# The place of one power on GpSimd's queue in the opening of a decoder layer

## The chip, the cores and the metric

The kernel runs on one core of a Trainium2 chip. The metric is the device time of one execution in microseconds (us). A core has five engines that each work through a queue of their own in order: TensorE (PE; its weight loads are listed as PEld), VectorE (DVE), ScalarE (ACT), GpSimd (POOL) and SyncE (SP), which issues most of the DMA transfers. Engines wait for each other by semaphores.

## The reference

One layer of a hybrid decoder on 256 tokens of width 1024, all in float32: two token mixers side by side on a normalised input, a gated merge, cross attention to 256 memory tokens, a gated MLP, and a last norm.

```python
xn = rmsnorm(h, norm_mix_g[l])
q_a, k_a, v_a, q_b, f_b, i_b, og_b, g_a, g_b = split_cols(xn @ w_in[l])
y_a = moba_attention(q_a, k_a, v_a, positions) @ w_br_attn[l]
y_b = hgrn2(q_b, f_b, i_b, og_b, lb_all[l], hgrn_norm_g[l]) @ w_br_hgrn[l]
merged = jax.nn.sigmoid(g_a) * y_a + jax.nn.sigmoid(g_b) * y_b
h = h + merged @ w_out[l]
h = h + memory_cross_attention(rmsnorm(h, norm_x_g[l]), rmsnorm(mem, norm_mem_g[l]),
                               wq_x[l], wkv_x[l], wo_x[l])
hn = rmsnorm(h, norm_ffn_g[l])
gu = hn @ w_ffn_in[l]
h = h + (jax.nn.silu(gu[..., :FFN_HIDDEN]) * gu[..., FFN_HIDDEN:]) @ w_ffn_out[l]
```

Two pieces matter here. `rmsnorm` multiplies each token by the reciprocal root of its mean square (its rstd), `x * rsqrt(mean(x*x) + 1e-6)`. The attention rotates its queries and keys by `cos` and `sin` of `position * inv_freq` (the rotary tables). The recurrence (`hgrn2`) has a forget gate `lb + (1 - lb) * sigmoid(f_b)`.

## The kernel before, in words

**Weights.** All weights lie in device memory as 97 units of 128 x 2048 values (1 MB), in the order in which they are used. `prep` takes one unit: SyncE loads it into `raw` (two buffers), ScalarE rounds it to `hi` (L189, in two halves of 128 x 1024; three buffers), and `lo = raw - hi` is made at L193, by VectorE alone for units 0 to 8 and from unit 9 on by VectorE (576 of 1024 columns) and GpSimd (448). A product with a weight takes three matmuls: hi with the high part of the input, lo with the high part, and hi with the low part (L233 to L235). `nxt` returns the next unit and prepares two more ahead of it. A raw buffer is free once the unit's lo is done, a hi buffer once TensorE has used it.

**Order.** TensorE's order is the program's. GpSimd's is the program's too in the region from the rotary generator's start to the end of the q gate (`manual_schedule` of Pool); elsewhere a scheduler orders the queues when the program is built. Work that runs beside the products is written as generators: `start` puts one on a list, and `tick`, called after each unit of a product, runs each of them up to its next `yield`.

**The opening.** Units 0 to 3 make the forget gate f: four accumulators `psg` (two column halves by two token halves of 128). The input's gain is applied, but not its rstd, as that is a factor for each token: it is applied where a product is read. To get it, ScalarE squares the tokens (H, loaded by SyncE) with a sum into `ssqx` (L516), VectorE makes mean + eps (`v_`, L282), and GpSimd raises it to the power -0.5 (L284, result `r_x`). VectorE halves it (`r_half`, L521), and ScalarE's tanh (`fth`, L467, four of them, one for each accumulator) reads an accumulator with it. TensorE turns the tanhs into `fT` (transposes, L445), and goes on with unit 4, the first of the q gate (accumulators `pst`, units 4 to 7), whose four evictions are `qth`. Then come `Vb` and `va` (units 8 to 15), and the attention's q and k, whose evictions (L725) read the rotary tables Ct and St.

**The rotary generator** `rope_tables` runs on GpSimd in parts with a `yield` between: the angle and its first reduction by multiples of 2 pi; a second part of five multiply-adds (`acc`, each L368 and L369) and a rounding (`rnd`, L363 to L365); a third of seven multiply-adds and some comparisons; a fourth of five operations; then four bare yields, two sines on ScalarE (L398, L399) and eight products with `r_x` that fill Ct and St (L403 to L405). The program drives the generator by hand at first: two `next` before the products, two more right behind the power,

```python
r_x = rstd_of(ssqx, "x")
next(rt)
next(rt)
r_half = cp.tile([128, 2], F32, name="r_half")
```

and then by ticks of the q gate, four in all, until `drain(rt)` ahead of the attention's q. GpSimd's products of neighbouring decays (Tt, L572) come behind the rotary chain in its queue.

Of the kernel before, what the change touches and what calls it, by code (L numbers as in the profile page):

```python
# [115 lines left out]
def build(tc, A, out):  # L116
    nc = tc.nc
    V, SC, G, PE, SY = nc.vector, nc.scalar, nc.gpsimd, nc.tensor, nc.sync
    with ExitStack() as ctx:
# [20 lines left out]
        def small(name, shape):  # L140
            return sp.tile([128] + list(shape), F32, name=name)
# [212 lines left out]
        def rope_tables():  # L354
            posf = small("posf", [2])
            G.tensor_copy(posf, posi)
            q = cp.tile([128, 7, 2, 32], F32, name="rt")
            ang, m, mh, ml, r, t, u = (q[:, i] for i in range(7))
            for i in range(2):
                G.tensor_scalar(ang[:, i], ifq, posf[:, i:i + 1], None, op0=ALU.mult)  # L360

            def rnd(o, src, c):
                G.tensor_scalar(o, src, c, None, op0=ALU.mult)  # L363
                G.tensor_scalar(o, o, RND, None, op0=ALU.add)
                G.tensor_scalar(o, o, RND, None, op0=ALU.subtract)  # L365

            def acc(o, a, c, b):
                G.tensor_scalar(u, a, float(c), None, op0=ALU.mult)  # L368
                G.tensor_tensor(o, u, b, op=ALU.add)  # L369

            rnd(m, ang, 1.0 / (TWO_PI * 1024.0))
            rnd(mh, m, 1.0 / 1024.0)
            G.tensor_scalar(mh, mh, 1024.0, None, op0=ALU.mult)
            G.tensor_tensor(ml, m, mh, op=ALU.subtract)
            yield 1
            acc(r, mh, -D1, ang)
            acc(r, ml, -D1, r)
            acc(r, mh, -D2, r)
            acc(t, ml, -D2, r)
            acc(t, mh, -D3, t)  # L380
            rnd(t, t, 1.0 / TWO_PI)
            yield 1
            for a, c in ((t, C1), (ml, D2), (mh, D3), (t, C2), (ml, D3), (t, C3), (m, D4)):
                acc(r, a, -c, r)
            lim = 3.1415925
            G.tensor_scalar(t, r, lim, -TWO_PI, op0=ALU.is_gt, op1=ALU.mult)
            G.tensor_scalar(ml, r, -lim, TWO_PI, op0=ALU.is_lt, op1=ALU.mult)
            G.tensor_tensor(r, r, t, op=ALU.add)
            G.tensor_tensor(r, r, ml, op=ALU.add)
            yield 1  # L390
            G.tensor_scalar(r, r, lim, -lim, op0=ALU.min, op1=ALU.max)
            G.tensor_scalar(t, r, 0.0, -2.0, op0=ALU.is_gt, op1=ALU.mult)
            G.tensor_scalar(t, t, 1.0, None, op0=ALU.add)
            G.tensor_tensor(t, t, r, op=ALU.mult)
            G.tensor_scalar(t, t, TWO_PI / 4, None, op0=ALU.add)
            for _ in range(4):
                yield 1
            tc.keep_in_program_order(SC.activation(m, r, AF.Sin))  # L398
            tc.keep_in_program_order(SC.activation(mh, t, AF.Sin))  # L399
            for i in range(2):  # L400
                rs = r_x[:, i:i + 1]
                for c in range(2):
                    G.tensor_scalar(Ct[:, i, c * 32:(c + 1) * 32], mh[:, i], rs, None, op0=ALU.mult)  # L403
                G.tensor_scalar(St[:, i, 0:32], m[:, i], rs, -1.0, op0=ALU.mult, op1=ALU.mult)
                G.tensor_scalar(St[:, i, 32:64], m[:, i], rs, None, op0=ALU.mult)  # L405

        rt = rope_tables()
        region = tc.manual_schedule(engines={mybir.EngineType.Pool})
        region.__enter__()
# [778 lines left out]
```

## Time and profile before

| | us |
|---|---|
| median of three runs | 632.65 |
| lowest and highest run | 631.9 and 633.71 |
| the profiled execution | 634.07 |
| its span, first to last instruction | 632.3 |
| mean granted TensorE clock | 0.994 |

A line of a timeline gives start and length in us, the engine, the line of the kernel, the operation, out<-in with partitions x elements, and how many instructions are merged; in brackets stands how long the engine was idle before and what ended that. A line of the chain gives start, length and what ran. A line of waits gives who waited for whom, the total in us, how often, and the longest. A line of stretches gives the stretch, its length, busy time and instructions of each engine asked for (PE, PEld, DVE, ACT, POOL), the granted clock as a share of full speed, the DMA engines' busy share and GB/s. Times count from the start of the span.

### The profile page before, as it was taken

What the parts mean: (1) busy time and instruction counts of PE and PEld (TensorE: products, weight loads), DVE (VectorE), ACT (ScalarE), POOL (GpSimd) and SP (SyncE); (2) the same over time, 40 slices, a digit from 0 to 9 for tenths busy, and PEclk for the clock granted to TensorE, in tenths of its full rate; (3) what the DMA queues carried; (4) which work ended last, traced back from release to release, by engine and by line L of the source; (5) the groups of instructions that cost most, each with busy time, mean ns of one, the idle gap of its engine ahead of it and who ended that gap; (6) DMA issues with size and microseconds to landing.
All of it is one profiled execution on the core that took longest, in us unless ns stands there. A gap on an engine that the chain in (4) does not pass through costs nothing.

```text
span 632.3 us, 8666 instructions
## 1 busy us (share of the span) xinstructions
PE 620.0 (98%) x3262; PEld 521.5 (82%) x3262; DVE 384.8 (61%) x649; ACT 325.1 (51%) x513; POOL 366.7 (58%) x287
## 2 busy tenths in 40 slices
PE   8899999999999999999999999999999999999995
PEld 6778888888887887778889999888888888888884
DVE  6475778889856875784656456754444444444433
ACT  5585544433377666773355444644544444444433
POOL 1897553466534564356865866646556655566542
PEclk9989999999999999999999999999999999999998
DMA  8655354443334433535454554562354554455511
GB/s 292 274 201 200 134 168 165 168 165 134 134 135 152 158 98 130 209 136 209 175 199 145 189 200 140 210 217 101 123 181 194 199 194 171 179 191 199 201 66 66
DMA packets 17321, 107.52 MB, mean 170 GB/s; under 512 B 2304, under 2 KB 2688, under 8 KB 4864
## 3 DMA queue, kind: packets, MB, share of 16 engines
q1 hardware_dynamic: 16704, 106.42, 47.1%
q10 hardware_dynamic: 576, 0.55, 0.3%
q8 instruction: 25, 0.41, 0.3%
q14 instruction: 16, 0.13, 0.1%
HBM read 105.92 MB, written 1.05 MB: 169 GB/s over the span
## 4 chain that ended last, share of the span: by engine, by line
PE 94%; issue 3%; POOL 2%; ACT 1%; DVE 0%; POOLq 0%; ACTq 0%
PE pst L233 14%; PE pst L235 14%; PE pst L234 14%; PE psi L233 6%; PE psi L235 6%; PE psi L234 6%; PE acc L235 3%; PE acc L234 3%; PE acc L233 3%; PE psf L229 2%; PE psf L228 2%; PE psf L230 2%; PE lp L600 2%; PE pso L233 1%; PE pso L235 1%
## 5 line engine op out<-in xcount | busy, mean ns | idle before, releaser
L193 POOL TENSOR_TENSOR lo<-raw,hi 128x448 fp32r<-128x448 f32 x172 | 269.9, 1583 | 196.7 <-ACT hi L189 193.7
L189 ACT ACTIVATE hi<-raw 128x1024 fp32r<-128x1024 f32 (+1 forms) x194 | 195.8, 1036 | 184.8 <-PE pst L235 67.8
L193 DVE TENSOR_TENSOR lo<-raw,hi 128x576 fp32r<-128x576 f32 (+2 forms) x194 | 198.1, 1028 | 126.5 <-ACT hi L189 125.3
L233 PE MATMUL pst<-hi,Xh 128*128 128x512 f32 x256 | 103.8, 406 | 0.0
L234 PE MATMUL pst<-lo,Xh 128*128 128x512 f32 x256 | 100.4, 392 | 0.0
L235 PE MATMUL pst<-hi,Xl 128*128 128x512 f32 x256 | 100.4, 392 | 0.0
L233 PE MATMUL psi<-hi,h2h 128*128 128x512 f32 x176 | 69.6, 395 | 0.0
L235 PE MATMUL psi<-hi,h2l 128*128 128x512 f32 x176 | 68.6, 390 | 0.0
L234 PE MATMUL psi<-lo,h2h 128*128 128x512 f32 x176 | 68.6, 390 | 0.0
L235 PEld LDWEIGHTS pst<-hi,Xl 128*128 128x128 f32 x256 | 48.5, 189 | 10.4
L233 PEld LDWEIGHTS pst<-hi,Xh 128*128 128x128 f32 x256 | 48.4, 189 | 10.0 <-issue 0.7
L234 PEld LDWEIGHTS pst<-lo,Xh 128*128 128x128 f32 x256 | 48.6, 190 | 9.2
L235 PEld LDWEIGHTS psi<-hi,h2l 128*128 128x128 f32 x176 | 33.0, 188 | 7.0
L233 PEld LDWEIGHTS psi<-hi,h2h 128*128 128x128 f32 x176 | 33.1, 188 | 6.6
L234 PEld LDWEIGHTS psi<-lo,h2h 128*128 128x128 f32 x176 | 33.1, 188 | 6.5
L233 PE MATMUL acc<-hi,hid 128*128 128x512 f32 x88 | 34.3, 390 | 0.0
L234 PE MATMUL acc<-lo,hid 128*128 128x512 f32 x88 | 34.2, 389 | 0.0
L235 PE MATMUL acc<-hi,hid 128*128 128x512 f32 x88 | 34.2, 389 | 0.0
L1075 DVE SCALAR_TENSOR_TENSOR fu<-psi,r_h,fg 128x256 f32<-128x256 f32 x22 | 10.6, 483 | 26.0 <-ACT fg L1073 26.0
L1073 ACT ACTIVATE fg<-psi,r_h 128x256 f32<-128x256 f32 x22 | 10.4, 475 | 29.9 <-PE psi L235 29.9
L235 PEld LDWEIGHTS acc<-hi,hid 128*128 128x128 f32 x88 | 16.5, 188 | 3.4
L234 PEld LDWEIGHTS acc<-lo,hid 128*128 128x128 f32 x88 | 16.5, 188 | 3.4
(338 smaller groups left out, 1174.5 us busy)
## 6 DMA issues: line engine op xcount, KB each, us to landing
raw<-w SPq DMA_DIRECT2D x95, 1024.0 KB, 4.8
raw<-w SPq DMA_DIRECT2D x8, 256.0 KB, 5.1
H<-xtok SPq DMA_DIRECT2D x1, 1024.0 KB, 9.4
mraw<-mT SPq DMA_DIRECT2D x1, 1024.0 KB, 7.0
out<-H SPq DMA_DIRECT2D x4, 256.0 KB, 2.2
xraw<-xT SPq DMA_DIRECT2D x2, 256.0 KB, 4.3
gfin<-gfin SPq DMA_DIRECT2D x1, 512.0 KB, 5.0
xraw<-xT ACTq DMA_DIRECT2D x2, 128.0 KB, 4.9
```

The source lines that it names most:

```text
L189: SC.activation(hi[:, a], raw[:, a], AF.Copy)
L193: eng.tensor_tensor(lo[:, b], raw[:, b], hi[:, b].bitcast(F32), op=ALU.subtract)
L228: PE.matmul(ps, lh, rh, start=first, stop=False)
L229: PE.matmul(ps, lh, rl, start=False, stop=False)
L230: PE.matmul(ps, ll, rh, start=False, stop=last)
L233: PE.matmul(ps, xh, h, start=first, stop=False)
L234: PE.matmul(ps, xh, l, start=False, stop=False)
L235: PE.matmul(ps, xl, h, start=False, stop=last)
L600: PE.matmul(ps[:, j], KS[:, a0 + j], QQ[:, a0 + j], start=True, stop=True)
L1073: SC.activation(g, ps[:, 0:256], AF.Silu, scale=r)
L1075: V.scalar_tensor_tensor(u, ps[:, 256:512], r, g, op0=ALU.mult, op1=ALU.mult)
```

## The change

One `yield` is put into the rotary generator behind the second of the five multiply-adds of its second part. The generator so has one part more. The two `next` ahead of the products now end behind two multiply-adds; the power of the tokens' rstd follows in GpSimd's queue; and the two `next` behind it run the other three multiply-adds with the rounding, and the third part. The parts that the ticks run come one tick later each: the sines and the tables Ct and St come with the first tick of `Vb` instead of the last of the q gate. The numbers of lines behind the yield grow by one.

```diff
             yield 1
             acc(r, mh, -D1, ang)
             acc(r, ml, -D1, r)
+            yield 1
             acc(r, mh, -D2, r)
             acc(t, ml, -D2, r)
             acc(t, mh, -D3, t)
             rnd(t, t, 1.0 / TWO_PI)
             yield 1
```

## The prediction

> **What bounds the kernel now.** I read the busy time of each engine first, then what TensorE waited for over the whole span.
>
> ```profile
> PE 620.0 (98%) x3262; PEld 521.5 (82%) x3262; DVE 384.8 (61%) x649; ACT 325.1 (51%) x513; POOL 366.7 (58%) x287
> PE fT__408 L445 <- ACT fth L467: 2.3, 2, 2.1
> PE warm L321 <- DVE still L318: 1.6, 1, 1.6
> PE psg L504 <- ACT hi L189: 0.7, 1, 0.7
> PE psg L504 <- ACT Xh L326: 0.3, 1, 0.3
> ```
>
> TensorE is busy 98% of the span, and the list of its waits has four entries in all, each of them in the opening. The largest, 2.3 us, is the first transposes of the forget gate (tiles fT), which wait for ScalarE's tanh (fth). After it TensorE waits for nobody, so every microsecond taken out here should come out of the end. Next I read the chain of work that ended last around that wait, and the timeline of each engine on it.
>
> ```profile
> 27.66 0.37 POOL rt L365
> 28.03 0.70 POOL r_x L284
> ...
> 32.23 0.55 PE fT__408 L445 x3
> ```
>
> ```profile
> 23.76 0.32 POOL L369 TENSOR_TENSOR rt<-rt 128x64 f32<-128x64 f32 x1
> ...
> 27.99 0.73 POOL L284 TENSOR_TENSOR r_x<-v__339,nhalf 128x2 f32<-128x2 f32 x1
> ```
>
> ```profile
> 24.04 0.17 DVE L282 TENSOR_SCALAR v__339<-ssqx 128x2 f32<-128x2 f32 x1 [1.85 <-ACT junk L516]
> 28.75 0.17 DVE L521 TENSOR_SCALAR r_half<-r_x 128x2 f32<-128x2 f32 x1 [4.54 <-POOL r_x L284]
> ```
>
> ```profile
> 23.83 0.19 ACT L516 ACTIVATION_READ_ACCUMULATOR junk<-H 128x1 f32 x1
> 29.02 0.69 ACT L467 ACTIVATE fth<-psg,r_half 128x512 f32<-128x512 f32 x1 [5.01 <-DVE r_half L521]
> 29.60 1.99 ACT L189 ACTIVATE hi<-raw 128x1024 fp32r<-128x1024 f32 x2
> 31.50 1.83 ACT L467 ACTIVATE fth<-psg,r_half 128x512 f32<-128x512 f32 x3
> ```
>
> The chain runs through GpSimd's rotary line (rt), the power (r_x), VectorE's halving of it (r_half) and the tanh. The power's input v is there at 24.04 + 0.17 = 24.21, but the power starts at 27.99: it stands in GpSimd's queue behind the second part of the rotary chain, and ScalarE idles 5.01 us for it. So 3.78 us of the latency of r_x is queueing alone.
>
> **The change, part by part.** No instruction is added or removed. The second part of the chain has five multiply-add pairs (L368, L369) and one rounding (L363 to L365). The new yield stands after the first two pairs, the second of which ends at 23.76 + 0.32 = 24.08. The power now follows, and the other three pairs and the rounding come behind it.
>
> *The power.* GpSimd gets to it at 24.08 and waits for v until 24.21, so it idles some 0.15 us; behind it in that queue stand only the remaining rotary operations. With 0.04 us to pass on (23.83 + 0.19 to 24.04 shows 0.02), the power runs 24.25 to 24.98. The first tanh came 29.02 - 27.99 = 1.03 after the power's start, so it starts at 25.28, 3.74 us earlier.
>
> *ScalarE behind it.* Its order stays: a tanh, two roundings of weight unit 4 (hi), then the three other tanhs. The transposes need the first two tanhs. The roundings need unit 4's weights.
>
> ```profile
> 19.65 0.33 SPq L183 DMA_DIRECT2D raw<-w  x1
> raw<-w SPq DMA_DIRECT2D x1, 1024.0 KB, 6.1
> 29.19 0.39 PE L235 MATMUL psg<-hi,Xl 128*128 128x512 f32 x1
> 30.68 2.48 DVE L193 TENSOR_TENSOR lo<-raw,hi 128x1024 fp32r<-128x1024 f32 x2 [1.76 <-ACT hi L189]
> ```
>
> The weights land at 19.65 + 6.1 = 25.75, just ahead of the rounding at 25.28 + 0.58 = 25.86. The second tanh, 31.50 - 29.02 = 2.48 after the first, starts at 27.76 and ends near 28.45. TensorE's last matmul of the f gate starts at 29.19 whatever happens here, so its transposes could start at 29.42: a spare of about 1 us, and the wait goes whole. What is late next is the fourth tanh: it needs that same matmul, so ScalarE waits until about 29.6 with the eviction of fT and unit 5's rounding behind it. ScalarE ends the tanhs near 30.3 instead of 33.33, some 3.0 us earlier. VectorE's lo of unit 4 (30.68, 1.08 after its first rounding) starts at 26.94 and is done by 29.42, before TensorE's first use.
>
> *TensorE.* Here I count by stretches: the columns are length, busy (instructions), granted clock, and DMA; the last row is one microsecond of the second stretch with all five engines, where the clock stands behind them.
>
> ```profile
> 29.42:32.96 3.54, 1.22 (x9) 1.00 0.00 0
> 32.96:40.15 7.19, 7.19 (x28) 0.76 0.60 218
> 40.15:40.94 0.79, 0.79 (x10) 1.00 1.10 467
> 40.94:51.92 10.98, 10.98 (x51) 1.00 0.59 210
> ```
>
> ```profile
> 34.00:35.00 1.00, 1.00 (x3) 0.79 (x3) 0.60 (x2) 1.00 (x2) 0.83 (x3) 0.50 0.44 98
> ```
>
> The stretch from 29.42 to 32.96 holds eight transposes and the wait. The next eight transposes, from 40.15, take 0.79 with nothing in the way. So the wait costs 3.54 - 0.79 = **2.75 us** (more than the 2.3 of the wait list, as the seams are in it). The 24 matmuls of unit 4 then take 7.19 us at a mean clock of 0.76; the 48 of units 5 and 6 take 10.98 at full clock, which makes 5.49 for 24. The difference, **1.70 us**, is the clock at half speed after the hole. With no hole I take it as gone too. Sum: 2.75 + 1.70 = 4.45 us.
>
> [...]
>
> *The steps that move behind.* The rotary generator now needs one tick more, so the two sines go behind the next weights' rounding and GpSimd's Ct and St behind four more lo operations.
>
> ```profile
> 59.04 0.25 ACT L398 ACTIVATE rt<-rt 128x64 f32<-128x64 f32 x1
> 63.23 4.98 POOL L193 TENSOR_TENSOR lo<-raw,hi 128x448 fp32r<-128x448 f32 x4
> L725 DVE TENSOR_TENSOR ra<-pst,Ct x8: 676/691/691, 123.9 to 167.8; 128x512 f32<-128x512 f32 x8
> ```
>
> The tables were full by 63.23, when GpSimd's next lo starts, and their first reader is at 123.9, 60 us later: this costs nothing, even if the tick comes 10 us late. The lo operations no longer queue behind the tables. No DMA moves in its queue.
>
> *Does the rest keep up?* TensorE would reach unit 5 at 29.42 + 0.79 + 5.49 + 0.79 = 36.49.
>
> ```profile
> 34.76 2.56 DVE L193 TENSOR_TENSOR lo<-raw,hi 128x1024 fp32r<-128x1024 f32 x2 [0.40 <-ACT hi L189]
> 38.35 1.99 ACT L189 ACTIVATE hi<-raw 128x1024 fp32r<-128x1024 f32 x2
> 53.57 1.16 POOL L193 TENSOR_TENSOR lo<-raw,hi 128x448 fp32r<-128x448 f32 x1
> 56.05 1.73 POOL L193 TENSOR_TENSOR lo<-raw,hi 128x448 fp32r<-128x448 f32 x1 [1.31 <-ACT hi L189]
> 65.74 0.53 PE L233 MATMUL pst<-hi,Xh 128*128 128x512 f32 x1
> ```
>
> Its lo ended at 37.32 and moves with ScalarE by 3.0 to 34.3: 2.2 us spare. Later units come faster than they are used: unit 4's rounding at 29.60 and unit 6's at 38.35 share a raw buffer, 8.75 us for two units or 4.4 for one, against 5.49. GpSimd is not sped up: its rotary and decay products still fill it until 53.57, where its first weights (unit 9) begin. Its two pieces then end by 53.57 + 1.16 + 1.73 = 56.5. TensorE uses unit 9 at 65.74, then at 61.3: 4.8 us spare.
>
> The profiled execution took 634.07 us with a span of 632.3, above the three runs' median of 632.65. The sum is made on that execution, and I take the same microseconds from the median: 632.65 - 4.45 = **628.2 us**.
>
> **The rivals.**
>
> *The clock's half-speed stretch stays, or the timed runs had none.* Then only 2.75 us come: 629.9. [...] Against it: the only stretch at 0.50 follows the only long hole behind the opening, and 580 us without such a hole stay at full clock:
>
> ```profile
> 52.00:632.00 580.00, 573.02 (x3061) 483.34 (x3059) 353.64 (x601) 290.97 (x461) 331.79 (x227) 1.00 0.46 163
> ```
>
> *No gain is kept.* A late supply of weights gives back all 4.45 us: 632.65. Unit 4 landing late would do part of it, 1 us for each us beyond the 1 us spare; unit 5 is the next narrow place (2.2 us). Against it: the margins above, and no wait on weights after the opening.
>
> *Slower: GpSimd slows when VectorE's lo runs beside more of its chain.*
>
> ```profile
> 30.99 1.09 POOL L369 TENSOR_TENSOR rt<-rt 128x64 f32<-128x64 f32 x1
> ```
>
> An addition takes 0.32 alone (23.76) and 1.09 beside the lo that starts at 30.68. The earlier tanh brings that lo forward by 3.74, onto operations that ran at 0.32 to 0.37. The slowing moves with it, and the chain grows only by as much lo as newly falls beside it: about one unit, two to four operations at 0.77, up to 3 us, inside the 4.8 spare. It decides from 4.8 us on, and to be slower than before the chain must grow by 4.8 + 4.45 = 9.3 us, twelve slowed operations more. If the slowing took 16 more, 12.3 us, TensorE would wait 7.5 at unit 9: 635.7. [...]
>
> That the power isn't moved can be left out: in the changed program it stands in GpSimd's queue ahead of the third pair.
>
> **How the numbers follow.** Forecast 0.62; half speed stays 0.24; nothing kept 0.09; slower 0.05. A measurement tells about 0.3% from no change, 1.9 us. The range takes the first two cases, each with the 1.06 us by which the highest run stands over the median: 628.2 - 1.1 = 627.1 to 629.9 + 1.1 = 631.0. Of the second case's 0.24 I leave 0.02 to runs that fall within 0.3%: faster 0.84, same 0.11, slower 0.05.
>
> **What would show it.** In the changed profile the power should start near 24.3 and the first tanh near 25.3; the wait of fT on fth should be gone; TensorE's first matmul of the q gate should start near 30.2, its 24 matmuls should take 5.5 us, and no slice near 33 us should show a lower clock. GpSimd's first lo should still start near 53.6. Wrong would be a new wait of TensorE on hi or lo at units 4, 5 or 9, or a tanh held by the landing of unit 4.

## The result, and the profile after

The changed kernel takes 629.64 us (median of five runs, 628.75 to 630.2) against 633.15 us of the kernel before (five runs, 631.9 to 633.71): a ratio of 0.995, with a 95% interval of 0.9934 to 0.9966. It is faster by some 3.2 us, clear of noise; forecast were 628.2 us, in a range of 627.1 to 631.0. The profiled execution of the changed kernel took 629.64 us with a span of 627.8, 4.4 us less than the profiled one of before.

First the engines' busy time and TensorE's waits in the profile after. The wait on the tanh is gone from the list; what is left lies ahead of the f gate's end.

```profile
PE 618.1 (98%) x3262; PEld 521.2 (83%) x3262; DVE 386.5 (62%) x649; ACT 324.9 (52%) x513; POOL 368.9 (59%) x287
PE warm L321 <- DVE still L318: 1.6, 1, 1.6
PE psg L234 <- DVE lo L193: 0.7, 1, 0.7
PE psg L505 <- ACT hi L189: 0.2, 1, 0.2
```

Then the timelines of GpSimd and of ScalarE. The power stands between the second and the third pair. It now starts as soon as v is there, where v had lain ready for 3.78 us before. The first tanh starts at 25.39, and the fourth waits 0.43 us for TensorE's last matmul.

```profile
22.68 0.32 POOL L369 TENSOR_TENSOR rt<-rt 128x64 f32<-128x64 f32 x1
24.36 0.73 POOL L284 TENSOR_TENSOR r_x<-v__330,nhalf 128x2 f32<-128x2 f32 x1 [1.36 <-DVE v__330 L282]
25.18 0.38 POOL L368 TENSOR_SCALAR rt<-rt 128x64 f32<-128x64 f32 x1
...
25.39 0.69 ACT L468 ACTIVATE fth<-psg,r_half 128x512 f32<-128x512 f32 x1 [1.31 <-DVE r_half L522]
26.00 2.01 ACT L189 ACTIVATE hi<-raw 128x1024 fp32r<-128x1024 f32 x2
27.92 1.25 ACT L468 ACTIVATE fth<-psg,r_half 128x512 f32<-128x512 f32 x2
29.59 0.69 ACT L468 ACTIVATE fth<-psg,r_half 128x512 f32<-128x512 f32 x1 [0.43 <-PE psg L235]
```

Last, TensorE by stretches (length, busy with instructions, granted clock, DMA share, GB/s): the eight transposes, unit 4, the next transposes, units 5 and 6.

```profile
29.40:30.19 0.79, 0.79 (x10) 1.00 0.00 0
30.19:35.73 5.54, 5.54 (x27) 1.00 0.62 204
35.73:36.52 0.79, 0.79 (x10) 1.00 0.65 259
36.52:47.50 10.98, 10.98 (x51) 1.00 0.72 262
```

Unit 5 starts at 36.52 instead of 40.94, which is 4.42 of the 4.5 us between the two spans. The first stretch was 3.54 and is 0.79; the second was 7.19 and is 5.54.

### The profile page after: what moved, and what is told of

Read it like the earlier page. It is cut to its first block, busy times and chain, and to the rows that moved or that the text cites. A ratio compares the mean times of both kernels' runs of the same rounds, so it can differ in the third digit from the quotient of the medians.

```text
span 627.8 us, 8666 instructions
## 1 busy us (share of the span) xinstructions
PE 618.1 (98%) x3262; PEld 521.2 (83%) x3262; DVE 386.5 (62%) x649; ACT 324.9 (52%) x513; POOL 368.9 (59%) x287
## 4 chain that ended last, share of the span: by engine, by line
PE 96%; DMA 2%; DVE 0%; SPq 0%; issue 0%; ACT 0%; POOLq 0%; POOL 0%
PE pst L233 14%; PE pst L234 14%; PE pst L235 14%; PE psi L233 6%; PE psi L235 6%; PE psi L234 6%; PE acc L235 3%; PE acc L234 3%; PE acc L233 3%; PE psf L229 2%; PE psf L228 2%; PE psf L230 2%; DMA raw<-w 2%; PE lp L601 2%; PE pso L233 1%; PE pso L235 1%
```

## The experiments

### What the median of the kernel before holds

The two profiles differ by 4.4 us, the medians by 3.5. So I ran the changed kernel again, with more runs of the kernel before beside it, and profiled the kernel before four more times (no edit).

> The changed kernel once more, as the measure for the others on this chip. Theory 1 (the wait of 2.75 us and the half-speed clock behind it both go): 4.0 to 4.5 us under the kernel before, granted clock of every run near 0.997 against 0.994. Theory 2 (the half-speed stretch comes in only some executions of the kernel before): 2.8 to 3.6 us under its median, and the single runs of the kernel before fall apart into two groups some 1.7 us from each other, with granted clocks near 0.994 and 0.997.

Measured: 630.39 us (six runs, 628.94 to 630.62) against 632.33 us of 21 runs of the kernel before; ratio 0.996, interval 0.9944 to 0.9975. All six show a granted clock of 0.997 or 0.998. The 21 runs of before fall apart by their clock: eight at 0.993 to 0.995 (633.11 to 633.95 us, median 633.7), ten at 0.997 or 0.998 (631.07 to 632.37, median 632.1), three at 0.996 between. The two groups are those of theory 2: their medians stand 1.6 us apart. The size is not: theory 2 expected 2.8 to 3.6 us under the median, and the medians differ by 1.9 us. The ratio makes it 2.5, with an interval from 1.6 to 3.5, so this set says little more of the size than that it is under the 4.45 of the sum.

> The kernel before, profiled once more, as a look at an execution of it without the half-speed stretch, if it comes so. Theory: with a granted clock of 0.997 or 0.998 in all, TensorE has the hole at the transposes as before, but its first 24 matmuls of the q gate take 5.5 us, and the time is near 632.1; with a clock of 0.993 to 0.995 they take 7.2 us, and the time is near 633.7. Rival (the two groups of runs differ elsewhere): the 24 matmuls take 7.2 us in a run of high clock, or 5.5 in one of low clock.

It came out with a clock of 0.994 and 633.47 us; the other three:

> The kernel before, profiled again, for an execution without the half-speed stretch. Theory: if the whole run's granted clock is 0.997 or 0.998, the hole at the transposes is there, the first 24 matmuls of the q gate take 5.5 us and the rest of the span from their start is 597.7 us; if it is 0.993 to 0.995, they take 7.2 us and the rest is 599.3.

> As the other profile of the kernel before: 24 matmuls in 5.5 us and a rest of 597.7 us with a high clock, 7.2 us and 599.3 with a low one.

> As the other profiles of the kernel before: 24 matmuls in 5.5 us and a rest of 597.7 us with a high clock, 7.2 us and 599.3 with a low one.

They took 632.36 us (clock 0.998), 631.02 (0.998) and 634.5 (0.993). Each pair of rows below shows the stretch from the start of the first transposes, or from the end of the f gate where these waited, to the q gate's first matmul, and then unit 4. In order: the runs labelled b, c (high clock), the first repeat and d (low clock).

```profile
29.91:32.79 2.88, 1.01 (x9) 1.00 0.00 0
32.79:38.33 5.54, 5.54 (x27) 1.00 0.66 207
```

```profile
28.76:31.54 2.78, 1.01 (x10) 1.00 0.00 0
31.54:37.08 5.54, 5.54 (x28) 1.00 0.72 209
```

```profile
29.25:32.35 3.10, 1.00 (x9) 1.00 0.00 0
32.35:39.55 7.20, 7.20 (x28) 0.76 0.67 218
```

```profile
29.84:33.38 3.54, 1.23 (x10) 1.00 0.00 0
33.38:40.53 7.15, 7.15 (x27) 0.76 0.61 211
```

Two things are to be seen. The half-speed stretch is not always there, as expected: 5.54 us with a high clock, 7.2 with a low one. And the hole, which is the first stretch less 0.79 for the transposes, is not 2.75 us in each execution: it is 2.09, 1.99, 2.31 and 2.75. The clock fell at the holes of 2.31 and 2.75, not at those of 1.99 and 2.09. From the q gate's first matmul to the end of the span the four take 597.8, 597.7, 599.4 and 599.3 us; the changed kernel takes 597.6. Without the 1.7 us of the low clock all five agree within 0.2 us, so nothing behind unit 4 differs.

### How long a hole lowers the clock

The power a little earlier than before: the yield behind the fifth pair.

```diff
             acc(t, mh, -D3, t)
+            yield 1
             rnd(t, t, 1.0 / TWO_PI)
             yield 1
```

> The yield stands behind the fifth multiply-add, so that the power goes ahead of the rounding only. The power should start at 26.7 instead of 27.99, 1.25 us earlier than in the kernel before; TensorE's hole at the transposes then shrinks by as much, from 2.75 to 1.5 us. If a hole of this length still lowers the clock: 1.25 us under the kernel before. If the clock falls only behind a longer hole: 1.25 + 1.70 = 2.95 us under it. The theory that the place of the power matters beyond its start has no number here; it would show as a start of the transposes that does not move with the power's.

Measured: 630.74 us (ten runs, 630.03 to 631.3), ratio 0.9968 (0.9957 to 0.9979). No run shows a clock below 0.996. Its power starts at 26.66, and the stretches are

```profile
29.64:31.69 2.05, 1.01 (x10) 1.00 0.00 0
31.69:37.25 5.56, 5.56 (x27) 1.00 0.62 200
```

The hole is 2.05 - 0.79 = 1.26 us, and the clock stays. Against the runs of before that kept their clock (632.1) it gains 1.4 us, near the 1.33 by which the power starts earlier. Of the two expected numbers neither is the median's (1.6), because the kernel before pays the clock only in part of its runs.

And the power later: behind the second of the seven multiply-adds of the third part.

```diff
             rnd(t, t, 1.0 / TWO_PI)
-            yield 1
-            for a, c in ((t, C1), (ml, D2), ...):
+            for j, (a, c) in enumerate(((t, C1), (ml, D2), ...)):
+                if j == 2:
+                    yield 1
                 acc(r, a, -c, r)
```

> The kernel before with the power put later: behind the first two of the seven multiply-adds of the third part, two pairs (some 1.7 us) behind its place in the kernel before. TensorE's hole at the transposes grows from 2.75 to some 4.5 us. Theory (the half-speed stretch comes by chance, and the more often the longer the hole; none in ten runs with a hole of 1.5 us, about eight of the 21 runs of the kernel before): the runs are 1.7 us slower by the hole, and most of them, over three in four, show a granted clock of 0.995 or less and 1.7 us more; median some 3 us over that of the kernel before. Rival (the half-speed stretch comes as often with any hole): 1.7 us over it, with four low clocks in ten runs.

Measured: 635.25 us (five runs), 2.75 above the kernel before on that chip (632.5, nine runs); ratio 1.0037 (1.0024 to 1.0051). Three of the five runs have a clock of 0.991 to 0.995, two 0.996. The profiled one (0.993):

```profile
28.96:34.38 5.42, 1.23 (x10) 1.00 0.00 0
34.38:41.52 7.14, 7.14 (x28) 0.76 0.65 219
```

The hole is 4.63 us (two waits of 2.05 and 2.14 us, with a transpose between them), and unit 4 takes 7.14. The median's 2.75 is near the expected 3. Over three in four low clocks were expected, and three of five came. Five runs don't settle the share (five of nine of the kernel before beside them were low too), so that the longer hole lowers the clock more often isn't shown by the count; that the short one did not in any run is (none in ten).

A third run put twelve matmuls into the wait.

```diff
             ev(t, pss[1][t])
+        fill = bank("fill")
+        for _ in range(12):
+            PE.matmul(fill, Xh[:, 0, 0:128], w[0][:, 0], start=True, stop=True)
         tick()
```

> The kernel before, with twelve more matmuls of 128x512 that nobody reads, put on TensorE between the f gate and its transposes, so that TensorE works through the time in which it waited. Theory 1 (the hole lowers the clock): the wait stays, as long as before (the transposes go on at about 32.2 us), but the 24 matmuls of unit 4 take 5.5 us instead of 7.2 in the profile; about 1.7 us under the kernel before, 2.7 above the changed one. Rival (the clock falls by its own timing at that place): unit 4 takes 7.2 us, no difference from the kernel before.

Measured: 634.03 us (twelve runs), ratio 1.0022 (1.001 to 1.0034): slower, not 1.7 us faster. Unit 4 does take 5.54 us, and no run has a clock below 0.996:

```profile
33.09:38.63 5.54, 5.54 (x27) 1.00 0.77 272
...
PE xT L1003 <- DVE xp L997: 0.6, 1, 0.6
```

But the rest from the q gate's first matmul is 598.7 us, 1.1 more than elsewhere, of which 0.6 is a wait that no other profile has. The other 0.5 I have not traced. And the filling is longer than the wait: the second tanh ends at 31.32, but the added matmuls run from 29.57 until the transposes at 32.29, so they hold the transposes back by some 0.9 us. The added matmuls also moved some weight roundings in ScalarE's and VectorE's queues, so this kernel is no clean test of the time. Of the clock it is one: with the hole filled, none of twelve runs is low, against eight of the 21 beside them.

### The spare, and the steps that moved behind

The yield behind the third pair instead of the second:

```diff
             acc(r, ml, -D1, r)
-            yield 1
             acc(r, mh, -D2, r)
+            yield 1
             acc(t, ml, -D2, r)
```

> The changed kernel with the yield one multiply-add later, so that the power starts at about 25.0 instead of 24.3. Theory (1 us of spare between the second tanh and the end of the f gate): no wait of TensorE at the transposes, the changed kernel's time within 0.5 us. Rival (the gain follows the power's start one for one): 0.7 to 0.9 us slower than the changed kernel.

Measured: 629.88 us (five runs), ratio 0.9955 (0.9943 to 0.9968), no wait at the transposes. This run did not test the spare: the power started at 24.69, held 0.49 us by v, and the f gate ended 0.31 us later too, so the power was ahead of it by as much as in the changed kernel (5.02 against 5.04 us).

The other profiles settle it. I call the time from the power's start to the end of the f gate (where the transposes could start) the power's lead:

| profile | power starts | f gate ends | lead | hole | lead and hole |
|---|---|---|---|---|---|
| late_power | 29.41 | 28.96 | -0.45 | 4.63 | 4.18 |
| before | 27.99 | 29.42 | 1.43 | 2.75 | 4.18 |
| before, d | 28.40 | 29.84 | 1.44 | 2.75 | 4.19 |
| before, first repeat | 27.38 | 29.25 | 1.87 | 2.31 | 4.18 |
| before, b | 27.81 | 29.91 | 2.10 | 2.09 | 4.19 |
| before, c | 26.56 | 28.76 | 2.20 | 1.99 | 4.19 |
| five_pairs | 26.66 | 29.64 | 2.98 | 1.26 | 4.24 |
| again | 24.28 | 28.64 | 4.36 | 0 | |
| three_pairs | 24.69 | 29.71 | 5.02 | 0 | |
| after | 24.36 | 29.40 | 5.04 | 0 | |
| same_tick | 23.05 | 28.92 | 5.87 | 0 | |

Lead and hole add up to 4.2 us wherever there is a hole, and from a lead of 4.36 on there is none. So the changed kernel's profile has a spare of some 0.8 us (1 us was forecast), and the hole of the kernel before varies because the lead does, from 1.4 to 2.2 us. Why the lead varies from one execution to the next I have not traced.

The changed kernel with the sines and tables at their old tick:

```diff
-            for _ in range(4):
+            for _ in range(3):
                 yield 1
```

> The changed kernel with three bare yields instead of four ahead of the sines, so that the sines and the tables Ct and St come at the same tick as in the kernel before; only the power's place is changed. If the later tick costs nothing: the changed kernel's time within 0.5 us. Rival (the four lo operations that no longer wait behind the tables are part of the gain, or the later tables cost something): over 0.5 us away from the changed kernel.

Measured: 629.86 us (six runs, 628.73 to 630.7) against 630.39 on the same chip, ratio to before 0.9953 (0.9937 to 0.9969). The difference of 0.53 us is a hair over the 0.5 that was to count for the rival, but the two sets of six runs span the same range (628.73 to 630.7 and 628.94 to 630.62): no cost and no gain of the later tick can be told from noise.

### The slower rival: where GpSimd's cover ends

```diff
             acc(r, ml, -D1, r)
             yield 1
+            for _ in range(24):
+                G.tensor_scalar(u, mh, 1.0, None, op0=ALU.mult)
             acc(r, mh, -D2, r)
```

> The changed kernel with 24 more GpSimd operations of 128x64 that change nothing, behind the power and ahead of the third multiply-add, so that GpSimd's chain ends some 11 us later: its first lo (unit 9) would start at 66 instead of 55.1. TensorE wants unit 9 at 61.3. Theory of the slower rival (spare of some 3.5 us, then one for one): a new wait of TensorE on GpSimd's lo of some 5 to 7 us, 634.5 to 637 us. Other theory (the chain's end has cover enough): no wait, the changed kernel's time.

Measured: 639.24 us (four runs), ratio 1.0103 (1.009 to 1.0117). It is over the 634.5 to 637 expected, and some 9.4 us over three_pairs (629.88), which stands in for the changed kernel on that chip. First GpSimd's first lo in the changed kernel, then in this one, and TensorE's two new waits:

```profile
55.07 5.51 POOL L193 TENSOR_TENSOR lo<-raw,hi 128x448 fp32r<-128x448 f32 x4
```

```profile
66.40 4.42 POOL L193 TENSOR_TENSOR lo<-raw,hi 128x448 fp32r<-128x448 f32 x4
...
PE pst L234 <- POOL lo L193: 4.7, 1, 4.7
PE l L557 <- ACT QQ L482: 2.2, 1, 2.2
ACT hi L189 <- DMA raw<-w: 16.6, 1, 16.6
...
68.00:69.00 1.00, 1.00 (x3) 0.73 (x3) 0.00 (x0) 0.00 (x0) 1.00 (x2) 0.50 0.00 0
```

The chain is 11.3 us late, TensorE waits 4.7 at unit 9: the spare is some 6.6 us. The wait is near the 5 to 7 us expected. Behind it come two costs that I had not priced: the raw buffers are freed late, so ScalarE waits 16.6 us for the next weights and TensorE 2.2 us for ScalarE's copies behind them in its queue; and the hole lowers the clock again (0.50). 4.7 + 2.2 and about half of some 3.3 us at half speed are 8.6 of the profile's 9.1 us over three_pairs (637.2 against 628.1); the last half microsecond I have not traced.

## Why the prediction was right, point by point

*The power and the tanh.* Forecast 24.3 and 25.3; they are at 24.36 and 25.39. GpSimd idled 1.36 us ahead of the power instead of 0.15, as its second pair ended at 23.00 instead of 24.08 in this execution; nothing waits for that.

*The wait goes whole.* Shown: no wait at the transposes, the q gate's first matmul at 30.19 (forecast 30.2), unit 4 in 5.54 us (5.5), unit 5 at 36.52 (36.49). Within the one execution on which the sum was made, both terms are right: 4.45 forecast, 4.4 between the profiles.

*The step that was mis-sized* is the last: "I take the same microseconds from the median". The profiled execution had the longest hole of the five profiles of the kernel before (2.75 us) and the half-speed stretch (1.70 us). In the five profiles of the kernel before the hole is 2.75, 2.31, 2.75, 2.09 and 1.99, mean 2.4, and the half-speed stretch comes in three of five, worth 1.0 on average: 3.4 us together, against the 3.5 between the medians and the 3.2 of the ratio. That agreement is in part luck: with the eight low clocks in 21 runs of the second set the same working gives 3.0, and that set measured 1.9 by the medians and 2.5 by the ratio.

*The rival with the half-speed stretch.* Its 629.9 us is nearer to the measured 629.64 than the forecast of 628.2. Its half "the timed runs had none" holds in part: ten of the 21 runs are clearly without it. Its other half, that the stretch stays in the changed kernel, is refuted: no run of the changed kernel, in either set, shows less than 0.996. Against this rival the prediction set 580 us at full clock. The 1.00 of that row is rounded: its last 4.4 us, behind TensorE's last matmuls, are at half speed (granted clock 0.79 in the microsecond from 627, 0.50 from 628 on).

*What hides the rest.* Weights kept up: no wait on unit 4, 5 or 9. The tables' first reader is at 119.5, after they are full, and the later tick makes no difference (same_tick). GpSimd's first lo came at 55.07 instead of the 53.6 forecast, 1.5 us late: some 0.3 by the wait for v and 1.2 by operations slowed while VectorE's lo ran (an addition at 27.36 took 1.14 us instead of 0.32). That is inside the "up to 3 us" of the slower rival, and cost nothing; that rival's threshold was set low (4.8 us behind the 53.6 forecast, against 6.6 behind 55.07, some 8.1 in all), and its price too low, as one for one left out the buffers and the clock.

## What to carry to other kernels

Where an engine's queue is in order, look at what stands ahead of the one small operation that the busiest engine waits for: moving it by a few places gave here all that could be had, with no instruction saved. A sum made on one profiled execution holds for that execution: before taking it from a median, profile the same kernel a few times and see whether the stall, and the clock behind it, are in each.

## What the runs showed of the hardware

TensorE's granted clock fell to 0.50 for 3.4 us at holes of 2.31, 2.75 and 4.63 us, and did not at 1.26, 1.99 and 2.09. The rows below are of the repeat with the 2.31 hole: the clock falls at 33.04 (0.52 as the mean of the microsecond), 0.69 us after the q gate's matmuls have started again, and stays down for 0.96 + 1 + 1 + 0.44 = 3.40 us.

```profile
33.00:34.00 1.00, 1.00 (x4) 0.76 (x3) 0.55 (x1) 1.00 (x3) 0.83 (x3) 0.52 1.02 131
34.00:35.00 1.00, 1.00 (x4) 0.76 (x3) 0.85 (x1) 1.00 (x3) 0.83 (x3) 0.50 0.52 221
35.00:36.00 1.00, 1.00 (x4) 0.81 (x3) 1.00 (x2) 1.00 (x3) 0.91 (x2) 0.50 1.01 426
36.00:37.00 1.00, 1.00 (x4) 0.79 (x4) 1.00 (x2) 0.03 (x1) 0.94 (x1) 0.78 0.65 270
```

The length of the hole alone does not decide. In pool_delay TensorE's second new wait is a hole of 2.40 us by the same measure (73.77 to 76.17), longer than 2.31, and the clock stays up behind it:

```profile
76.00:77.00 1.00, 0.83 (x5) 0.83 (x6) 1.00 (x2) 1.00 (x4) 1.00 (x2) 1.00 0.00 0
77.00:78.00 1.00, 1.00 (x7) 0.96 (x6) 1.00 (x3) 1.00 (x4) 1.00 (x1) 1.00 0.00 0
78.00:79.00 1.00, 1.00 (x6) 0.78 (x5) 0.98 (x2) 1.00 (x3) 1.00 (x3) 1.00 0.00 0
```

What decides beside the length was not shown. That it is where in time a hole lies is my estimate from these two holes, and no run tested it. What is shown is that one kernel pays in some executions only: the kernel before in three of its five profiles, at holes of 2.31, 2.75 and 2.75 us.

Two falls came while TensorE still stood: in pool_delay at 67.44, inside the 4.7 us wait at unit 9 that ends at 67.58, and in the profile of before at 627.58, behind its last matmul, which starts at 624.64.

```profile
67.00:68.00 1.00, 0.42 (x1) 0.42 (x2) 0.00 (x0) 0.00 (x0) 1.00 (x2) 0.72 0.00 0
```
